# Block sums of weights on VectorE, normed rows kept in memory, layer 1's modulation weights in the row buffers

## The chip, the cores and the metric

The kernel runs on one core of one Trainium2 chip. The metric is the device time of one execution in microseconds; the time before is the median of three runs. The profile is of one further execution, recorded by the hardware profiler. A core has TensorE (PE; its weight loads are listed as PEld), VectorE (DVE), ScalarE (ACT), GpSimd (POOL) and SyncE (SP), which here only issues DMAs.

## The reference

Two layers of a diffusion backbone in fp32 work on 256 context tokens and 1024 latent tokens with 1024 features. Per layer `i`, for the latent tokens (the context tokens the same with their own modulation, and not at all after layer 0):

```python
mod = silu(c) @ ada_w[i] + ada_b[i]                  # 6 sections: sh1, sc1, g1, sh2, sc2, g2
h = x * (1 + sc1) + sh1
m = mixers(h)                                        # GLA, retention, latent attention
x = layer_norm(ALPHA * x + g1 * (m @ w_out), ln1)
u = conv3((x * (1 + sc2) + sh2) @ ffn_up)            # 1024 -> 2 x 2816, a convolution over 3 tokens
f = (silu(u[:2816]) * u[2816:]) @ ffn_down
x = layer_norm(ALPHA * x + g2 * f, ln2)
```

The modulation weights `ada_w[i]` are 1024 x 6144, so 24 MB per layer for a product with two vectors.

## The kernel before

Activations lie transposed: features on the partitions, tokens along the free axis, so 1024 features are 8 row blocks "k". Every fp32 product is made of three fp32r products: each operand is split into a rounded part (a cast on ACT, L255) and the remainder (a subtraction on VectorE, L256), by `split`. Weights are split too, when they are used.

Per layer come the projection, the mixers, the output projection (`wout`), and then the feed-forward stage, which the change touches. The tokens go through it in two parts (`PARTS`, L78): 644 and 636 tokens in layer 0, 512 and 512 in layer 1. The hidden features are 22 blocks of 128, twice (a and g).

- **Up** (`ffn_up`, L1214). One call makes the blocks f (A) and NF + f (G) of the up projection for one part as one 2x2 block product with seven instead of eight multiplications. It needs sums of blocks of the weights (`wload`, L202: x and z, four additions of 128x512 on GpSimd, L218) and sums of blocks of the tokens (`sums`, L1178, the operand X). Seven `product` calls (L1238, matmuls L1242) go through PSUM banks 0 to 3. VectorE and ACT evacuate them (L1251, L1260, L1264, L1257, L1267), then the convolution (L1281 to L1283) and the gate (L1286, L1287) follow, and the result is split.
- **Down** (`ffn_down`, L1292). After three up blocks (first after one) their share of the down projection goes through PSUM banks 4 to 7 (matmuls L1318), is scaled by ACT (L1328) and added to the rows `yd` in memory by a DMA that GpSimd issues (L1330). The order of the calls is in `ffn_order` (L43): a down group follows the first up block of the next group.
- **Background work.** `net.bg` is a list of generators. `tick` advances the first of them, a step or two after every up call and one per step of a down group. After the output projection it holds the LayerNorm of part 1 (`ln`, L1106), in layer 0 then layer 1's modulation (`ada`, L291), and later the second LayerNorm of part 0.
- **Layer 1's modulation** (`ada`). Each of six sections loads eight tiles of 128x1024 (L301), multiplies each with the two vectors (L306, into bank 7, which is also a down bank), and then copies, transposes and stores the section (L310, L314, L319). Before a down group, an unfinished section is brought to its end (`while net.ada_on`).

Buffers are shared by tag: `wst` has 4 slots of 4 KB per partition, for weights as they arrive (A, G, down weights, and the modulation weights). `y` has 8 slots of 5 KB: the rows before and after the first LayerNorm (four slots for each part; those of part 0 are given up when X is made), half of X's split operands (two slots), the block sums x and z (two slots per up block). Part 1's rows, once normed, are stored to `yd` (L1147) and also stay in their `y` slots. `modulate` (L332, on VectorE at L340) scales and shifts them there in place; it is put into the background list at up block 20 of part 0 (`stage[1]`, L1505), and its end is waited for before part 1's first up block (L1499).

The program text does not fix the order on an engine: a scheduler in the framework puts each engine's instructions in order by the text's order, operands and free slots, and then each engine works through its list in that order. The list is fixed before the run.

Of the kernel before, what the change touches and what calls it, by code (L numbers as in the profile page):

```python
# [42 lines left out]
def ffn_order(l):  # L43
    out, pend = [], None
    for part in range(2):
        for gi, (f0, gn) in enumerate(groups(l, part)):
            for f in range(f0, f0 + gn):
                out.append(("up", part, f))
                if pend:
                    out.append(("down",) + pend)  # L50
                    pend = None
            pend = (part, gi)
    return out + [("down",) + pend]
# [7 lines left out]
def groups(l, part):  # L61

    out, f = [], 0
    for n in [1] + [3] * 7:
        out.append((f, n))
        f += n
    return out
# [15 lines left out]
class Net:  # L83
# [118 lines left out]
    def wload(self, i):  # L202

        nc, (src, shape) = self.nc, self.wq[i]
        if not isinstance(src, tuple):
            t = self.ws(shape)
            nc.sync.dma_start(t[:], src)
            self.wst[i] = t
        elif shape == PAIR[0]:
            l, _, f = src  # L210
            A, G = self.ws([128, 8, 128]), self.ws([128, 8, 128])
            nc.sync.dma_start(A[:], self.a["up"][l, f])
            nc.sync.dma_start(G[:], self.a["up"][l, NF + f])
            x, z = self.yk(shape=(128, 2, 4, 128)), self.yk(shape=(128, 2, 4, 128))
            lo, hi = slice(0, 4), slice(4, 8)
            for out, p, q, op in ((x[:, 0], G[:, lo], G[:, hi], ALU.add), (x[:, 1], x[:, 0], A[:, lo], ALU.subtract),
                                  (z[:, 0], A[:, lo], G[:, lo], ALU.subtract), (z[:, 1], A[:, hi], x[:, 1], ALU.subtract)):
                nc.gpsimd.tensor_tensor(out, p, q, op=op)  # L218
            self.wsum[src] = {0: (A, A[:, lo]), 1: (A, A[:, hi]), 2: (z, z[:, 1]), 3: (G, G[:, hi]), 4: (x, x[:, 0]), 5: (x, x[:, 1]), 6: (z, z[:, 0])}

    def wahead(self):
# [1161 lines left out]
def kernel(ctx: ExitStack, tc: tile.TileContext, a, out):  # L1383
    net = Net(ctx, tc, a)
    nc = tc.nc
# [4 lines left out]
    for l in range(NL):  # L1390
# [10 lines left out]
        if l == 0:  # L1401
# [23 lines left out]
            ada = net.after(net.ada(0, [(None, s) for s in (2, 3, 4, 5)]))  # L1425
# [29 lines left out]
        y = [net.ytiles(c1 - c0) for c0, c1 in parts]  # L1455
        yd = net.dp.tile([128, 8, T], F32, name=f"y{l}")

        def residual(part):
            F = []
            c0, c1 = parts[part]  # L1460
            get = net.loader(S.m, c0, c1)
            for k in range(8):
                f = net.hid([128, 644])
                F.append(get(k, f))
                nc.sync.dma_start(y[part][k], xsrc[:, k, c0:c1])
            return F

        P = [net.ffn_part(l, i) for i in range(2)]
        lns = [net.ln(l, p.c0, p.c1, y[p.part], V_LN1G, V_LN1B, (yd, 0)) for p in P]
        Ff = [[], []]  # L1470
        stage = [net.modulate(l, 3, p.c0, p.c1, lambda k, f, p=p: y[p.part][k], Ff[p.part], here=True) for p in P]
        F = residual(0)
        h = net.hsplit(F, parts[0][1] - parts[0][0])
        F1 = residual(1)
# [11 lines left out]
        X = net.sums(Ff[0], P[0].c1 - P[0].c0)  # L1486
        Ff[0] = y[0] = None
        net.after(lns[1])
        if l == 0:
            ada = net.after(net.ada(1, [(None, s) for s in range(6)]))  # L1490
        nx = None
        F = []
        store = [(net.xs, 0), (out, CTX)][l]
# [1 line left out]
        for op, part, x in ffn_order(l):  # L1495
            p = P[part]
            if op == "up":
                if part and x == 0:
                    net.drain(stage[1])  # L1499
                    X = net.sums(Ff[1], p.c1 - p.c0)  # L1500
                    Ff[1] = y[1] = None
                net.ffn_up(l, p, x, X)
                net.tick(2 if ada in net.bg else 1)
                if part == 0 and x == 20:
                    net.bg.insert(0, stage[1])  # L1505
            else:
                while net.ada_on:
                    net.tick()
                for _ in net.ffn_down(l, p, x, yd):
                    net.tick(1, but=ada)  # L1510
                if part == 0 and x == len(groups(l, part)) - 1:
                    net.bg.insert(0, ln2[0])
                if part and x == len(groups(l, part)) - 2:
                    if l == 0:
                        net.drain(ln2[0])
                        nx = net.modulate(1, 0, 0, 640, net.loader(net.xs, 0, 640), F)
                        for _ in nx:
                            pass
                    else:
                        d0, d1 = p.done  # L1520
                        p.Y = net.ytiles(d1 - d0)
                        for k in range(8):
                            nc.sync.dma_start(p.Y[k], yd[:, k, d0:d1])
# [103 lines left out]
```

## Time and profile before

| | us |
|---|---|
| median of 3 runs | 3760.41 (3749.32 to 3762.21) |
| the profiled execution | 3756.62 |
| its span, first to last instruction | 3754.8 |
| TensorE matmuls busy | 3381.9 (90%) |
| TensorE weight loads busy | 2951.0 (79%) |
| VectorE busy | 2710.2 (72%) |
| ACT busy | 1909.6 (51%) |
| GpSimd busy | 1160.8 (31%) |

Layer 0's feed-forward lies at about 940 to 2060 us of the span, layer 1's at about 2870 to 3740. A busy share is a mean over stages with different limits. In a group of instructions "mean ns of one" is the mean duration; what stands behind the second bar is the idle time of that engine just before these instructions, and what ended it. TensorE's busy time is modelled from pipelined matmuls and grows when its granted clock is low.

### The profile page before, as it was taken

The numbers are of one execution on the slowest core, as the hardware profiler recorded it, in microseconds if no ns is written. First come the engines' busy times: TensorE is split into PE (matmuls) and PEld (weight loads), VectorE is DVE, ScalarE is ACT, GpSimd is POOL, SyncE is SP. The second block draws the span as 40 slices with busy tenths as digits, with TensorE's granted clock in tenths as the row PEclk, the third lists the DMA queues.
The fourth block names the chain that finished last, engine by engine and source line by source line (L and its number), as shares of the span: only waits on it lengthen the run. The fifth ranks groups of instructions, "written<-read, shape, count | busy, mean of one in ns | idle before, by whom it ended". The sixth has DMA issues, their size and how long they took to land. (4 is left out here: it accounts for less than half of the span.)

```text
span 3754.8 us, 63790 instructions
## 1 busy us (share of the span) xinstructions
PE 3381.9 (90%) x24510; PEld 2951.0 (79%) x24510; DVE 2710.2 (72%) x4501; ACT 1909.6 (51%) x3785; POOL 1160.8 (31%) x1227
## 2 busy tenths in 40 slices
PE   7999999999888878788998899999998799888997
PEld 6887667679777768688998898767687688787997
DVE  3335878776886655677877744878869899978885
ACT  3334555553454444456555544555545555655554
POOL 0000334330343323235342100333303554445443
PEclk9999999999899988899999999999999999999998
DMA  7554111223345556465455644111232555455553
GB/s 270 174 184 125 37 52 40 75 88 112 94 131 141 146 138 147 110 144 132 119 124 142 217 133 137 32 53 47 66 121 90 132 135 132 113 152 132 122 135 91
DMA packets 223986, 447.60 MB, mean 119 GB/s; under 512 B 20992, under 2 KB 115008, under 8 KB 223680
## 3 DMA queue, kind: packets, MB, share of 16 engines
q1 hardware_dynamic: 187968, 370.11, 30.3%
q0 software_dynamic: 35712, 73.41, 12.8%
q8 instruction: 192, 3.15, 0.3%
q14 instruction: 114, 0.93, 0.1%
HBM read 319.45 MB, written 119.27 MB: 117 GB/s over the span
## 5 line engine op out<-in xcount | busy, mean ns | idle before, releaser
L256 DVE TENSOR_TENSOR w<-ws,w 128x512 fp32r<-128x512 f32 (+2 forms) x476 | 479.1, 1007 | 397.9 <-ACT w L255 137.7
L1242 PE MATMUL ps<-h,w 128*128 128x256 f32 (+2 forms) x4224 | 648.8, 305 | 114.7 <-DVE u L1251 37.3
L1242 PEld LDWEIGHTS ps<-h,w 128*128 128x128 f32 x4224 | 598.4, 195 | 141.4 <-DVE u L1251 44.6
L1318 PE MATMUL ps<-hid,w 128*128 128x256 f32 (+4 forms) x3696 | 615.7, 327 | 60.4 <-ACT t L1328 47.5
L1318 PEld LDWEIGHTS ps<-hid,w 128*128 128x128 f32 x3696 | 567.7, 199 | 98.7 <-ACT t L1328 55.8
L366 PE MATMUL ps<-h,w 128*128 128x320 f32 (+4 forms) x3264 | 549.2, 327 | 11.9 <-ACT h L255 6.3
L366 PEld LDWEIGHTS ps<-h,w 128*128 128x128 f32 x3264 | 509.3, 191 | 52.8 <-issue 15.4
L255 ACT CAST w<-ws 128x512 fp32r<-128x512 f32 (+2 forms) x476 | 361.9, 761 | 259.0 <-PE ps L366 99.8
L1008 POOL TENSOR_SCALAR dg<-ident,sm 128x128 f32<-128x128 f32 x144 | 99.8, 698 | 961.8 <-DVE sm L1006 840.2
L256 DVE TENSOR_TENSOR w<-y,w 128x512 fp32r<-128x512 f32 x352 | 302.6, 864 | 97.0 <-ACT w L255 95.4
L1242 PE MATMUL ps<-hid,w 128*128 128x256 f32 (+2 forms) x2112 | 335.3, 308 | 15.8 <-ACT t L1257 9.5
L962 PE MATMUL ps<-h,h 96*128 96x512 f32 (+1 forms) x1200 | 321.8, 389 | 18.3 <-DVE w L990 13.4
L1242 PEld LDWEIGHTS ps<-hid,w 128*128 128x128 f32 x2112 | 308.6, 199 | 26.8 <-ACT t L1257 11.8
L1330 POOL DMA_DIRECT2D y<-t x248 | 222.2, 1015 | 306.2 <-ACT t L1328 303.8
L255 ACT CAST w<-y 128x512 fp32r<-128x512 f32 x352 | 216.8, 617 | 163.7 <-POOL y L218 72.3
L1328 ACT ACTIVATE t<-ps,mod 128x256 f32<-128x256 f32 (+6 forms) x432 | 211.1, 535 | 113.7 <-PE ps L1318 62.1
L975 ACT ACTIVATE w<-ps,sm 128x768 f32<-128x768 f32 (+2 forms) x272 | 209.1, 774 | 111.5 <-DVE sm L971 89.5
L962 PEld LDWEIGHTS ps<-h,h 96*128 96x128 f32 x1200 | 197.7, 192 | 77.4 <-issue 21.0
L218 POOL TENSOR_TENSOR y<-ws 128x512 f32<-128x512 f32 x88 | 136.4, 1550 | 373.1 <-DMA ws<-in_up_dram 282.9
L988 PE MATMUL ps<-ident,w 128*128 128x128 f32 x1312 | 219.8, 284 | 12.2 <-ACT w L975 11.9
L1281 ACT ACTIVATE t<-u,vec 128x644 f32<-128x644 f32 (+3 forms) x176 | 153.3, 871 | 134.7 <-DVE u L1251 118.0
L988 PEld LDWEIGHTS ps<-ident,w 128*128 128x128 f32 x1312 | 149.7, 142 | 71.1 <-issue 34.6
(225 smaller groups left out, 5538.1 us busy)
## 6 DMA issues: line engine op xcount, KB each, us to landing
ws<-in_up_dram SPq DMA_DIRECT2D x176, 512.0 KB, 4.0
ws<-in_down_dram SPq DMA_DIRECT2D x112, 384.0 KB, 3.2
ws<-in_ada_dram SPq DMA_DIRECT2D x80, 512.0 KB, 3.9
ws<-in_w_in_dram SPq DMA_DIRECT2D x48, 512.0 KB, 4.5
y<-t POOLq DMA_DIRECT2D x64, 321.5 KB, 5.4
y<-t POOLq DMA_DIRECT2D x64, 318.5 KB, 7.4
ws<-in_w_out_dram SPq DMA_DIRECT2D x32, 512.0 KB, 3.4
y<-t POOLq DMA_DIRECT2D x64, 255.5 KB, 6.4
```

Source lines behind the costliest of these rows:

```text
L218: nc.gpsimd.tensor_tensor(out, p, q, op=op)
L255: self.nc.scalar.copy(hi, src)
L256: self.nc.vector.tensor_tensor(lo, src, hi.bitcast(F32), op=ALU.subtract)
L366: nc.tensor.matmul(ps[:, i, 0:n], w_[:, k, :], h[k][:, part, o:o + n], start=(k == 0 and q == 0), stop=(k == 7 and q == 2))
L962: nc.tensor.matmul(sc[:, o:o + n], q[qa][0:96, qs], K[ka][0:96, o:o + n], start=(x == 0), stop=(x == 2))
L975: nc.scalar.activation(P[:, c0:c1], sc[:, c0:c1], AF.Exp, bias=st[:, 2:3], scale=MSCALE, accum_out=st[:, 3 + j:4 + j])
L988: nc.tensor.transpose(ps[:, t_], P[:, 128 * (t0 + t_):128 * (t0 + t_) + 128], self.ident[:])
L1242: nc.tensor.matmul(bank[:, 0:w], w_[:, k, :], X[i][k][:, part, :], start=(first and k == 0 and q == 0), stop=(k == 3 and q == 2), skip_gro ...
L1281: nc.scalar.activation(v[:, 0:n], u[:, 1:1 + n], AF.Identity, scale=cw(j, 1), bias=self.vec[l][:, V_CB + j:V_CB + j + 1])
L1318: nc.tensor.matmul(pb[i][:, 0:n], w[w_][:, x, ms], p.hh[f0 + x][hp][:, o - 1:o - 1 + n], start=(x == 0 and q == 0), stop=(x == gn - 1 and ...
L1328: nc.scalar.activation(t[:, cd - base:cd - base + n], pb[i][:, o:o + n], AF.Identity, scale=self.md(l, 5, m, who))
L1330: nc.gpsimd.dma_start(yd[:, m, base:base + e], t[:, 0:e], accum_op=ALU.add)
```

## The change

Three edits. The four block sums of a weight pair are instructed on VectorE instead of GpSimd. Part 1's normed rows are no longer kept in `y` slots from the LayerNorm on: their tiles are given up when the LayerNorm has stored them, and a new step at block 20 takes four new `y` slots, loads the rows from `yd` with eight DMAs on SyncE, and modulates them there. Layer 1's modulation weights are loaded into `y` slots instead of `wst` slots.

```diff
@@ wload
-                nc.gpsimd.tensor_tensor(out, p, q, op=op)
+                nc.vector.tensor_tensor(out, p, q, op=op)
@@ tile_hybrid_kernel
-        stage = [net.modulate(l, 3, p.c0, p.c1, lambda k, f, p=p: y[p.part][k], Ff[p.part], here=True) for p in P]
+
+        def second():
+
+            p = P[1]
+            Y = net.ytiles(p.c1 - p.c0)
+            for k in range(8):
+                nc.sync.dma_start(Y[k], yd[:, k, p.c0:p.c1])
+            yield
+            yield from net.modulate(l, 3, p.c0, p.c1, lambda k, f: Y[k], Ff[1], here=True)
+
+        stage = [net.modulate(l, 3, P[0].c0, P[0].c1, lambda k, f: y[0][k], Ff[0], here=True), second()]
@@
         net.after(lns[1])
+        lns, y[1] = None, None
         if l == 0:
-            ada = net.after(net.ada(1, [(None, s) for s in range(6)]))
+            ada = net.after(net.ada(1, [(None, s) for s in range(6)], alloc=lambda s: net.yk(shape=s)))
@@
                     X = net.sums(Ff[1], p.c1 - p.c0)
-                    Ff[1] = y[1] = None
+                    Ff[1] = None
```

## Rows read from the trace of the kernel before

**Rows 1.** The page's first part: busy us, share of the span, instructions.
```profile
PE 3381.9 (90%) x24510; PEld 2951.0 (79%) x24510; DVE 2710.2 (72%) x4501; ACT 1909.6 (51%) x3785; POOL 1160.8 (31%) x1227
```
**Rows 2.** Feed-forward stretches: us, busy PE, PEld, DVE, ACT, POOL; PEclk, DMA share, GB/s.
```profile
940.00:2060.00 1120.00, 959.79 (x6201) 906.46 (x6200) 804.21 (x1171) 564.04 (x995) 407.08 (x432) 0.92 0.53 130
2870.00:3740.00 870.00, 758.81 (x5334) 708.40 (x5335) 744.23 (x1114) 496.07 (x904) 400.94 (x439) 0.95 0.52 125
```
**Rows 3.** The same for one group each: layer 0 parts 0, 1; layer 1 parts 0, 1.
```profile
1227.00:1306.30 79.30, 67.47 (x465) 61.87 (x464) 48.49 (x70) 35.42 (x64) 26.63 (x32) 0.91 0.58 147
...
1881.90:1943.40 61.50, 59.24 (x400) 58.47 (x399) 46.00 (x65) 34.42 (x60) 26.42 (x26) 1.00 0.51 120
...
3176.80:3226.40 49.60, 47.12 (x326) 43.43 (x325) 44.70 (x65) 29.72 (x52) 25.45 (x32) 1.00 0.54 137
...
3553.30:3606.40 53.10, 48.81 (x401) 47.81 (x400) 44.56 (x65) 31.44 (x60) 25.05 (x26) 1.00 0.56 131
```
**Rows 4.** TensorE's waits, 1147.6 to 1590: us in total, times, longest.
```profile
PE ps L306 <- DMA ws<-in_ada_dram: 66.2, 24, 4.0
```
**Rows 5.** TensorE in order of time, one section: start, us, instructions, idle before.
```profile
1155.74 0.64 PE L306 MATMUL ps<-ws,st 128*32 128x256 f32 x8 [2.41 <-DMA ws<-in_ada_dram]
1160.27 1.08 PE L306 MATMUL ps<-ws,st 128*32 128x256 f32 x8 [3.88 <-DMA ws<-in_ada_dram]
...
1166.65 0.69 PE L314 MATMUL ps<-ident,t 128*128 128x128 f32 x2 [0.49 <-ACT t L310]
```
**Rows 6.** SyncE's queue in order of time, the same section.
```profile
1147.70 14.04 SPq L301 DMA_DIRECT2D ws<-in_ada_dram  x4
```
**Rows 7.** Line 218: min/median/max ns of the first sum; what ended its idle time.
```profile
L218 POOL TENSOR_TENSOR y<-ws x88: 1256/1322/3196, 958.6 to 3678.6; 128x512 f32<-128x512 f32 x88
...
  DMA ws<-in_up_dram: 282.9, 52
```
**Rows 8.** Line 256, min/median/max ns, of the split of block sums.
```profile
L256 DVE TENSOR_TENSOR w<-y,w x352: 671/684/3949, 963.6 to 3691.7; 128x512 fp32r<-128x512 f32 x176
```
**Rows 9.** All engines in order of time, around one block sum in layer 1.
```profile
3143.16 1.57 POOL L218 TENSOR_TENSOR y<-y,ws 128x512 f32<-128x512 f32 x1
...
3143.24 2.05 DVE L256 TENSOR_TENSOR w<-y,w 128x512 fp32r<-128x512 f32 x1
```
**Rows 10.** VectorE's groups of the whole run: busy us, mean ns, idle before.
```profile
L256 DVE TENSOR_TENSOR w<-y,w 128x512 fp32r<-128x512 f32 x352 | 302.6, 864 | 97.0 <-ACT w L255 95.4 <-PE ps L1242 0.7
L1283 DVE SCALAR_TENSOR_TENSOR t<-u,vec,t 128x644 f32<-128x644 f32 (+3 forms) x176 | 189.7, 1078 | 1.1
L1282 DVE SCALAR_TENSOR_TENSOR t<-u,vec,t 128x644 f32<-128x644 f32 (+3 forms) x176 | 184.1, 1046 | 12.3 <-ACT t L1281 11.1
```
**Rows 11.** VectorE's groups by form, feed-forward of layer 0, then of layer 1.
```profile
L256 DVE TENSOR_TENSOR w<-ws,w 128x512 fp32r<-128x512 f32 x132 | 115.6, 876 | 93.1 <-ACT w L255 91.9
...
L256 DVE TENSOR_TENSOR w<-ws,w 128x512 fp32r<-128x512 f32 x131 | 124.3, 949 | 41.7 <-ACT w L255 41.5
```
**Rows 12.** Line 1282: min/median/max ns.
```profile
L1282 DVE SCALAR_TENSOR_TENSOR t<-u,vec,t x176: 731/877/1997, 987.5 to 3702.6; 128x644 f32<-128x644 f32 x44, 128x638 f32<-128x638 f32 x44, 128x512 f32<-128x512 f32 x44, 128x514 f32<-128x514 f32 x44
```
**Rows 13.** TensorE's waits for evacuations on VectorE, whole run.
```profile
PE ps L1242 <- DVE u L1251: 37.3, 38, 4.2
PE ps L1242 <- DVE t L1260: 31.1, 15, 7.2
```
**Rows 14.** Line 340, modulation: min/median/max ns, first and last start; idle until.
```profile
L340 DVE TENSOR_SCALAR hid<-hid,mod x48: 405/474/615, 17.4 to 2166.4; 128x256 f32<-128x256 f32 x16, 128x384 f32<-128x384 f32 x16, 128x640 f32<-128x640 f32 x16
L340 DVE TENSOR_SCALAR y<-y,mod x40: 397/532/2223, 939.5 to 3036.1; 128x512 f32<-128x512 f32 x16, 128x256 f32<-128x256 f32 x8, 128x388 f32<-128x388 f32 x8, 128x636 f32<-128x636 f32 x8
...
  DMA hid<-xs: 15.2, 7
  DMA hid<-in_xT_dram: 7.7, 4
```
**Rows 15.** DMA issues: KB each, median us from issue to landing, of normed rows.
```profile
y<-y SPq DMA_DIRECT2D x8, 318.5 KB, 5.7
```

## The prediction

> **What bounds the kernel now.** I read the page's engine totals first [rows 1]: TensorE is busy 90% of the span, VectorE 72%, GpSimd 31%. All three edits act in the feed-forward stages, so the second view is the busy time by stretch over these two stages [rows 2]: VectorE is busy 804 of 1120 us in layer 0 and 744 of 870 us in layer 1. The third view is the same table for single groups, each of three up blocks and one down group [rows 3]. In layer 0 a group of part 0 takes 79.3 us, one of part 1 61.5 us. Both compute the same; the group of part 0 also carries one section of layer 1's modulation weights (L306). Its TensorE is busy 67.5 us and idle 11.8, at a granted clock of 0.91; in part 1 it is 59.2 us busy and 2.3 idle, at 1.00. In layer 1 the groups take 49.6 us (47.1 busy) and 53.1 us (48.8 busy), so a steady group there has only 2.5 to 4.3 us to win.
>
> Then the waits of TensorE [rows 4] and one section in order of time [rows 5]. The reader is to see L306 waiting up to 3.88 us for each of its loads, and on SyncE's queue four of these loads in a row that lasts 14 us [rows 6]: a load waits until the matmuls of the one before have released the staging slot, then takes about 3.9 us, then come about 1 us of matmuls, four times. Over the six sections the wait is 66.2 us in 24 pieces. This is the one large stall that repeats.
>
> **Edit 3, layer 1's modulation weights in the y buffers.** There are 8 y slots. In part 0 the split operands of the running part (X) hold two, the block sums of one up block two, and part 1's normed rows four. Edit 2 frees those four until they are reloaded, so that after LayerNorm six slots serve block sums and modulation weights. When a section is drained, two hold the next block's sums, which leaves up to four for the four loads that now go one after another. They need no longer wait for matmuls, and the staging slots are left to the feed-forward weights.
> - Wait removed: 66.2 us [rows 4].
> - Clock: the section's own TensorE work at full clock is 8 x 0.64 + 0.69 = 5.8 us [rows 5]; the busy time of its group is 67.5 - 59.2 = 8.3 us over that of a group without [rows 3]. The 2.5 us between I put down to the stretch of lower clock that follows the stall (1.08 us against 0.64 for the same eight matmuls): 15 us in six sections.
> - Ceiling: 66 + 15 = 81 us. Check by the groups' lengths: 6 x (79.3 - 61.5 - 5.8) = 72 us.
> - Given back: the first matmul of a section needs the PSUM bank that the down group before it uses, so weights loaded too early sit in slots that the next block's sums want. I charge one load per section, 3.88 x 6 = 23 us, from the ceiling, which leaves 58; I take **60 us gained**. Ends: 20 us (half the loads still in series, and the sums late) and 81 us.
>
> **Edit 1, block sums on VectorE.** 88 up blocks with 4 sums each are 352 instructions of 128x512. On GpSimd the quickest kind has a median of 1.32 us [rows 7]. VectorE does the same shape between SBUF operands in a median of 0.684 us (L256, w<-y) [rows 8], so it gains 352 x 0.684 = 241 us of work.
> What it sheds is seen in [rows 9]: the same subtraction takes 2.05 us while a sum runs on GpSimd. Means against undisturbed lengths, over the whole run: w<-y 352 x (864 - 684) ns = 63 us [rows 8, 10]; w<-ws of 128x512 132 x (876 - 684) + 131 x (949 - 684) ns = 60 us [rows 11]; the convolution steps L1282 and L1283, half of them about 512 wide (shortest 731 ns) and half about 640 (for these I take the median, 877, so 804 on average [rows 12]), 176 x (1046 + 1078 - 2 x 804) ns = 91 us [rows 10]. That is 214 us, without L1287, the LayerNorm's and others. VectorE's total thus rises by at most 27 us.
> [...]
> On the path are VectorE's evacuations: TensorE waits 37.3 + 31.1 = 68 us for L1251 and L1260 [rows 13]. They lose the slow-downs and get blocks of sums in front of them instead; I take 20 us as gain. Against it, a sum waits for its weight load. On GpSimd that wait (282.9 us in 52 pieces [rows 7]) cost nothing; on VectorE, which works through its queue in order, the evacuations and weight splits stand behind it, and TensorE waits for both. The trace has no such wait on VectorE. Its nearest instructions are the modulations behind loads: 15.2 + 7.7 us over 48 of them [rows 14], 0.48 us each, times 88 is 42 us, of which I let a third, 15 us, reach TensorE, as VectorE idles 442 us in the two stages [rows 2]. Net: **5 us gained**. Ends: 41 us gained (if the lines left out shed another 68 us, so 282 less 241, all on the path) and 110 us lost (rival C).
>
> **Edit 2, part 1's rows wait in memory.** Eight more loads of 318 KB in layer 0 and 256 KB in layer 1, 5.7 us each to landing [rows 15], on SyncE's queue among the weight loads, and one more step of the background work. The rows' store exists already. The framework issues an instruction when its operands and slots allow, not where the text has it: part 1's modulation stands at block 20, yet the last of them began at 3036.1 [rows 14], with groups of part 0 running past 3226 [rows 3]. So in layer 1, where no modulation weights want the slots, I expect the reload at once after the LayerNorm, and then the state of before. In layer 0 the modulation weights come first. Hidden by some 190 us of feed-forward, the reload costs **0**. Without that cover it is one batch per layer, 2 x (5.7 + 8 x 0.53 us of modulation [rows 14]) = 20 us lost; the other end is 10 us gained, if the sums get a second pair of slots for a while and one wait per group of layer 1's part 0 is halved.
>
> **Sum.** 60 + 5 + 0 = 65 us. The profiled execution took 3756.6 us (span 3754.8 and 1.8 around it), 3.8 us under the median of 3760.4 and within the runs' 3749.3 to 3762.2. 3756.6 - 65 = **3692 us**.
>
> **Rivals.**
> - A, the slots are fought over: modulation weights and block sums take turns on the y slots, and loads stay in series. For it: 6 slots for up to 4 sum tiles and 8 loads of a section, and early issue. Against it: six is more than the one staging slot in use now. It gives the low end of edit 3: 3757 - 20 - 5 = 3732 us.
> - B, more than forecast: the whole stall goes (81) and VectorE's net relief is all on the path (41): 3757 - 122 = 3635 us. For it: TensorE's short waits are on VectorE [rows 13]. Against it: [rows 3] leave steady groups only 2.5 to 4.3 us.
> - C, VectorE becomes layer 1's bound. It now idles 126 us there [rows 2]; 44 blocks bring 44 x 4 x 0.684 = 120 us. If the relief does not come, or is eaten by waiting for loads, the idle time, which is waiting in order, does not fill up and the stage grows by up to 120 us; layer 0 keeps its gain less 10. 3757 - 60 + 120 + 10 = 3827 us; halfway, 3767. It decides from the point where 65/88 = 0.74 us of delay per up block reaches TensorE. For it: the tight row of layer 1 in [rows 2]. Against it: [rows 9].
> - D, the change does not do what it says: the reloaded rows take the four slots back before the modulation weights can use them, so that these compete with the sums for two. 3757 +- 15 us. Against it: in the kernel's text the modulation weights stand before the reload, so they are served first.
>
> **How the numbers follow.** Forecast (3660 to 3725) 0.55, A 0.10, B 0.12, C 0.14, D 0.09. The range 3640 to 3770 leaves out part of B (0.07) and most of C (0.12). A difference of 0.5%, 19 us, is what a measurement of this kernel can tell from none: faster is below 3742. Forecast, A and B are there, 0.77; D is the same, with a little of C, 0.10; the rest of C is slower, 0.13.
>
> **What would show it.** Right: TensorE's wait of L306 for modulation loads in layer 0's feed-forward falls from 66 to under 25 us; groups of part 0 last 66 to 70 us, with the clock near 1.00; SyncE issues L301 without the 14 us row. w<-y at a mean near 0.69 us, with VectorE's total busy time within 40 us of 2710; GpSimd under 700 us. Layer 1's groups within 2 us of 49.6 and 53.1. Wrong: VectorE waiting for up-weight loads by more than 60 us in total, or layer 1's groups longer by over 2 us (C); L306 still waiting more than 45 us (A or D); the sums waiting for slots that modulation weights hold.

## The result, and the profile after

The changed kernel takes 3664.74 us (median of 4 runs, 3663.23 to 3669.04) against 3761.31 for the kernel before on the same chip: a ratio of 0.975, 95% interval 0.9727 to 0.9774. It is 97 us faster. The forecast of 3692 us was 27 us too slow; the range held the time. Its total came near by errors that offset each other; of its terms only edit 3's came near in size, and that with the sums still on GpSimd, as the experiments show.

The page of the kernel after, first part, answers to [rows 1]:

```profile
PE 3371.0 (92%) x24510; PEld 2954.0 (81%) x24510; DVE 2631.2 (72%) x4853; ACT 1916.0 (52%) x3785; POOL 618.0 (17%) x875
```

VectorE took over 352 instructions and yet is 79 us less busy than before. The same feed-forward stages by stretch, as in [rows 2]:

```profile
940.00:1990.00 1050.00, 949.68 (x6227) 901.58 (x6226) 778.65 (x1352) 568.98 (x999) 129.55 (x256) 0.95 0.55 142
2800.00:3655.00 855.00, 762.01 (x5354) 719.13 (x5353) 695.46 (x1295) 501.48 (x905) 141.77 (x264) 0.94 0.54 130
```

Single groups, as in [rows 3]: layer 0 part 0 twice, layer 0 part 1, layer 1 part 0, layer 1 part 1.

```profile
1144.60:1217.40 72.80, 67.69 (x464) 62.32 (x463) 46.91 (x82) 35.22 (x64) 7.67 (x20) 0.93 0.60 160
1217.40:1288.20 70.80, 67.25 (x464) 62.68 (x464) 46.98 (x82) 35.27 (x64) 7.66 (x20) 0.95 0.61 164
1816.60:1877.00 60.40, 58.62 (x399) 58.09 (x398) 45.48 (x77) 34.67 (x60) 7.51 (x14) 1.00 0.54 122
...
3107.50:3160.60 53.10, 48.92 (x325) 45.67 (x325) 41.39 (x77) 30.27 (x52) 7.70 (x20) 0.94 0.56 129
3424.70:3476.70 52.00, 48.59 (x396) 48.38 (x395) 41.77 (x77) 31.47 (x60) 7.52 (x14) 0.97 0.57 131
```

Three groups are shorter than before; the group of layer 1's part 0 is 3.5 us longer (53.1 against 49.6), at a granted clock of 0.94 where it was 1.00. What it waits for is in VectorE's waits of the kernel after; the kernel before has no such row on VectorE:

```profile
DVE y L218 <- DMA ws<-in_up_dram: 149.5, 53, 7.3
```

And in order of time, in layer 1's part 0:

```profile
3027.35 0.69 DVE L218 TENSOR_TENSOR y<-ws 128x512 f32<-128x512 f32 x1 [4.90 <-DMA ws<-in_up_dram]
...
3030.36 0.42 DVE L1251 TENSOR_TENSOR u<-ps,t 128x256 f32<-128x256 f32 x1
...
3030.84 1.65 PE L1242 MATMUL ps<-h,w 128*128 128x256 f32 x6 [4.60 <-DVE u L1251]
```

The first sum of a block stands at the head of VectorE's list and waits 4.9 us for its weights. The evacuation L1251 stands behind it, with two more sums and two splits between, and TensorE waits 4.6 us for that evacuation. The pattern returns in five groups there: TensorE waits 4.0 to 4.7 us for L1251 at 2978.1, 3030.8, 3084.2, 3136.3 and 3189.4 us, and in none of the groups before.

TensorE's waits after, during layer 1's modulation in layer 0's feed-forward (1090 to 1530 us), and of the whole run:

```profile
PE ps L306 <- DMA y<-in_ada_dram: 21.7, 25, 3.1
```

```profile
PE ps L1242 <- DVE u L1251: 47.3, 19, 4.8
...
PE ps L1242 <- DVE t L1260: 25.3, 16, 4.6
PE ps L1318 <- ACT t L1328: 16.9, 14, 2.8
```

The modulation loads cost 21.7 us where they cost 66.2 [rows 4]; the first section reads so in order of time, against [rows 5]: one load is still waited for, and three are all but there.

```profile
1149.56 0.64 PE L306 MATMUL ps<-y,st 128*32 128x256 f32 x8 [0.34 <-DMA y<-in_ada_dram]
1153.33 1.08 PE L306 MATMUL ps<-y,st 128*32 128x256 f32 x8 [3.13 <-DMA y<-in_ada_dram]
1154.61 1.08 PE L306 MATMUL ps<-y,st 128*32 128x256 f32 x8 [0.20 <-DMA y<-in_ada_dram]
1155.86 1.08 PE L306 MATMUL ps<-y,st 128*32 128x256 f32 x8 [0.17 <-DMA y<-in_ada_dram]
```

### The profile page after: what moved, and what is told of

The parts are those of the page before. It is cut to its first block, busy times and chain, and to the rows that moved or that the text cites. A ratio compares the mean times of both kernels' runs of the same rounds, so it can differ in the third digit from the quotient of the medians.

```text
span 3667.3 us, 63639 instructions
## 1 busy us (share of the span) xinstructions
PE 3371.0 (92%) x24510; PEld 2954.0 (81%) x24510; DVE 2631.2 (72%) x4853; ACT 1916.0 (52%) x3785; POOL 618.0 (17%) x875
## 5 line engine op out<-in xcount | busy, mean ns | idle before, releaser
L1242 PE MATMUL ps<-h,w 128*128 128x256 f32 (+2 forms) x4224 | 651.2, 306 | 104.9 <-DVE u L1251 47.3
L1242 PEld LDWEIGHTS ps<-h,w 128*128 128x128 f32 x4224 | 605.1, 197 | 125.5 <-DVE u L1251 52.5
L256 DVE TENSOR_TENSOR w<-ws,w 128x512 fp32r<-128x512 f32 (+2 forms) x476 | 411.0, 865 | 342.2 <-PE ps L366 146.0
L1318 PE MATMUL ps<-hid,w 128*128 128x256 f32 (+4 forms) x3696 | 600.8, 323 | 34.1 <-ACT t L1328 16.9
L1242 PE MATMUL ps<-hid,w 128*128 128x256 f32 (+2 forms) x2112 | 338.8, 309 | 22.4 <-ACT t L1257 13.0
L1242 PEld LDWEIGHTS ps<-hid,w 128*128 128x128 f32 x2112 | 311.5, 200 | 33.4 <-ACT t L1257 14.4
L1330 POOL DMA_DIRECT2D y<-t x248 | 215.2, 896 | 472.8 <-ACT t L1328 470.7
L256 DVE TENSOR_TENSOR w<-y,w 128x512 fp32r<-128x512 f32 x352 | 240.6, 688 | 36.9 <-ACT w L255 34.1
L1328 ACT ACTIVATE t<-ps,mod 128x256 f32<-128x256 f32 (+6 forms) x432 | 209.2, 534 | 105.3 <-PE ps L1318 65.6
L1225 POOL MEMSET u<- 128x1 f32 (+1 forms) x264 | 27.3, 156 | 1151.3 <-DVE t L1283 811.0
```

Of the source, the lines that this page charges most:

```text
L256: self.nc.vector.tensor_tensor(lo, src, hi.bitcast(F32), op=ALU.subtract)
L1242: nc.tensor.matmul(bank[:, 0:w], w_[:, k, :], X[i][k][:, part, :], start=(first and k == 0 and q == 0), stop=(k == 3 and q == 2), skip_gro ...
L1318: nc.tensor.matmul(pb[i][:, 0:n], w[w_][:, x, ms], p.hh[f0 + x][hp][:, o - 1:o - 1 + n], start=(x == 0 and q == 0), stop=(x == gn - 1 and ...
L1328: nc.scalar.activation(t[:, cd - base:cd - base + n], pb[i][:, o:o + n], AF.Identity, scale=self.md(l, 5, m, who))
L1330: nc.gpsimd.dma_start(yd[:, m, base:base + e], t[:, 0:e], accum_op=ALU.add)
```

## The experiments

All were timed against the kernel before (3760 to 3762 us in each set) on one chip per set. "Shift" below is how much earlier (negative) an up block begins than in the kernel before, in the profiled runs: the start of the L1242 matmul that stands at n/88 of that line's records. The 88 up blocks are counted from 0 in order of time: block 22 is the first of layer 0's part 1, block 44 the first of layer 1, block 66 the first of its part 1. "End" is the end of the span. Each row is one profiled run.

| shift, us | block 22 | block 44 | block 66 | end |
|---|---|---|---|---|
| edit 1 alone | -8.5 | -29.4 | -52.9 | -78.4 |
| edit 2 alone | +9.0 | +10.9 | +14.3 | +7.7 |
| edits 1 and 2 | -15.8 | -28.3 | -21.1 | -48.4 |
| edits 2 and 3 | -37.9 | -50.3 | -40.5 | -43.9 |
| all three | -44.2 | -67.3 | -59.8 | -87.6 |
| all three, every third block's sums on GpSimd | -51.1 | -82.4 | -90.4 | -117.6 |
| all three, edit 2 in layer 0 only | -47.4 | -74.5 | -101.9 | -128.6 |
| both | -58.3 | -98.1 | -111.5 | -139.1 |

**One edit, or two.** The first four runs took the change apart. Edit 3 without edit 2 was not tried: the rows that stay and the modulation weights want the same slots.

Edit 1 alone:

```diff
-                nc.gpsimd.tensor_tensor(out, p, q, op=op)
+                nc.vector.tensor_tensor(out, p, q, op=op)
```

> Edit 1 alone (block sums on VectorE; rows and modulation weights as before). Before 3761 us, after 3665 us. Theory S (the serial loads of modulation weights are most of the gain, about 70 of 97 us): about 3740 us; L306 still waits about 66 us in layer 0's feed-forward, w<-y falls to a mean of 0.69 us, VectorE waits over 100 us for up weights. Theory P (the GpSimd contention is most of it): 3700 us or less, with layer 0's groups of part 0 at 75 us or less instead of 79.3.

Measured: 3676.66 us, ratio 0.9775 (0.9752 to 0.9799), 84 us faster by itself. Theory S fell. Theory P had the time, but not the place: up to layer 0's part 1 the run gains only 8.5 us. TensorE's waits of the kernel before, and then of this one:

```profile
PE ps L1318 <- ACT t L1328: 47.5, 28, 6.1
...
PE ps L1242 <- DVE t L1264: 18.3, 18, 2.4
```

```profile
PE ps L306 <- DMA ws<-in_ada_dram: 81.5, 43, 4.1
PE ps L1242 <- DVE t L1260: 26.4, 16, 4.0
PE ps L1318 <- ACT t L1328: 17.4, 13, 2.2
PE ps L1242 <- DVE u L1251: 16.9, 8, 3.7
...
PE ps L1242 <- DVE t L1264: 5.1, 3, 4.1
```

With [rows 13], four waits lose 30 (L1328), 20 (L1251), 13 (L1264) and 5 us (L1260): 68 us. TensorE's busy time falls as well, from 3381.9 to 3369.4 us, and some other waits are longer; the spans differ by 78 us. The sums wait 67.8 us for weights on VectorE, and little of it shows in the evacuations.

Edit 2 alone (the diff of the change without its first line pair and without `alloc=`):

> Edit 2 alone (part 1's rows reloaded; sums on GpSimd, modulation weights through the staging slots). Theory S: 3761 within 8 us, since the reload is hidden and freed slots alone start nothing that was late. Theory Q (the freed slots let the block sums run a pair ahead): 3740 us or less, and GpSimd's sums wait less for w L256.

Measured: 3765.08 us, ratio 1.0015 (0.9999 to 1.0031): no change.

Edits 1 and 2:

```diff
-            ada = net.after(net.ada(1, [(None, s) for s in range(6)], alloc=lambda s: net.yk(shape=s)))
+            ada = net.after(net.ada(1, [(None, s) for s in range(6)]))
```

> Edits 1 and 2, without edit 3. Theory S: about 3735 us, so that edit 3 is worth about 70 us on top; L306 waits about 66 us. Theory P: 3690 us or less. Theory Q: 20 us or more below edit 1 alone.

Measured: 3701.83 us, 0.9848 (0.9824 to 0.9871). None of the theories had named this time. Edit 2, which costs nothing alone, costs 25 us beside edit 1. The table says where: from block 44 to 66, edit 1 alone gains 23.5 us, and both together lose 7. In that stretch this kernel has five of the stalls for L1251 shown above (4.1 to 4.7 us each), and edit 1 alone has none. VectorE's waits for up weights, edit 1 alone and edits 1 and 2:

```profile
DVE y L218 <- DMA ws<-in_up_dram: 67.8, 29, 6.8
...
DVE y L218 <- DMA ws<-in_up_dram: 120.8, 40, 6.9
```

Edits 2 and 3, sums on GpSimd:

```diff
-                nc.vector.tensor_tensor(out, p, q, op=op)
+                nc.gpsimd.tensor_tensor(out, p, q, op=op)
```

> Edits 2 and 3, block sums still on GpSimd. Theory S: about 3690 us; layer 0's groups of part 0 fall from 79.3 to about 72 us, layer 1's part 0 stays at 49.6 us per group (the 52.5 us of after come from the sums on VectorE waiting for weights). Theory P: 3730 us or more.

Measured: 3709.95 us, 0.9868 (0.9833 to 0.9903), 55 us less than edit 2 alone, between what the two theories had named. Edit 3's gain arrives before block 44. From block 44 to 66 this kernel loses 10 us and edit 2 alone 3, so a small part of edit 2's loss there may not need the sums on VectorE. TensorE's wait for L1328 is 45.5 us here, as before the change, so its fall belongs to edit 1.

So edit 1 gives 84, edit 3 55 and edit 2 loses 5; the sum would be 134, and the change has 97. Edit 3's part shrinks too: beside edits 1 and 2 it is worth 37 us (3701.83 against 3664.74).

**What the sums on GpSimd cost.** The changed kernel with twelve additions per up block on GpSimd (three after each sum), whose results nothing reads:

```diff
+                for j in range(3):
+                    nc.gpsimd.tensor_tensor(self.dgt()[:], G[:, j], A[:, j], op=ALU.add)
```

> The changed kernel, with twelve idle additions of 128x128 per up block put on GpSimd beside the sums on VectorE (their results are not used; they read the same weights). This brings back GpSimd's traffic and nothing else. If GpSimd's additions slow VectorE's: w<-y rises from a mean of 0.69 to 0.8 us or more, VectorE's busy time by 100 us or more over 2631, and the time to 3690 us or more. If GpSimd's traffic does not matter: all three stay within 1%.

Measured: 3857.8 us, 1.0251 (1.0234 to 1.0267), 193 us over the changed kernel. GpSimd's busy time is 1389.9 us, VectorE's 2844.2, which is 213 more than after, for the same instructions. Its groups of VectorE (lines two further on than after: L258 is L256, L1284 is L1282):

```profile
L258 DVE TENSOR_TENSOR w<-ws,w 128x512 fp32r<-128x512 f32 (+2 forms) x476 | 445.1, 937 | 337.2 <-PE ps L368 138.9 <-ACT w L257 72.9 <-PE ps L499 64.3
L258 DVE TENSOR_TENSOR w<-y,w 128x512 fp32r<-128x512 f32 x352 | 266.9, 762 | 38.7 <-ACT w L257 37.4 <-PE ps L1244 0.2
```

The same groups after:

```profile
L256 DVE TENSOR_TENSOR w<-ws,w 128x512 fp32r<-128x512 f32 (+2 forms) x476 | 411.0, 865 | 342.2 <-PE ps L366 146.0 <-ACT w L255 76.0 <-PE ps L497 63.9
L256 DVE TENSOR_TENSOR w<-y,w 128x512 fp32r<-128x512 f32 x352 | 240.6, 688 | 36.9 <-ACT w L255 34.1 <-PE ps L1242 1.3
```

Beside work on GpSimd that nobody needs, VectorE's instructions took those 213 us more, though the mean of w<-y, 762 ns, stays under the 800 that were expected. TensorE's wait for L1328 rises to 70.9 us as well, so this run does not separate the slowing of VectorE from the accumulating DMAs (L1330) that stand behind the sums in GpSimd's list. One run takes away the length and keeps GpSimd's wait for the weights:

```diff
+            nc.gpsimd.tensor_tensor(self.dgt()[:, 0:1], G[:, 0, 0:1], A[:, 0, 0:1], op=ALU.add)
```

> The changed kernel with one more instruction on GpSimd per up block: an addition of 128x1 that reads the first column of both weight tiles, into a tile that nothing reads. It makes GpSimd's list wait for the weights' landing, as the sums did before the change, and takes next to no time on the memory that VectorE uses. Theory 1: a good part of edit 1's gain is that the accumulating DMAs (L1330) no longer stand behind a GpSimd that waits for weights; then TensorE's wait of the down matmuls (L1318) for ACT's scaling (L1328) rises from 16.9 towards 47.5 us, and the time by 20 to 30 us, to 3685 to 3695 us. Theory 2: what GpSimd's sums cost was their running time, beside VectorE and in front of those DMAs; then the wait stays under 25 us and the time within 8 us of 3665 us.

Measured: 3679.12 us, 0.979 (0.9771 to 0.981), 14 us over the changed kernel's run, in another set. GpSimd's row and TensorE's waits (lines one further on than after):

```profile
POOL dg L219 <- DMA ws<-in_up_dram: 660.3, 82, 86.1
```

```profile
PE ps L1243 <- DVE u L1252: 58.6, 19, 6.2
...
PE ps L1319 <- ACT t L1329: 19.7, 14, 4.7
```

GpSimd waits for weights far longer than it did before the change (282.9 us [rows 7]), and TensorE's wait for ACT's scaling rises only from 16.9 to 19.7. Theory 1 falls: waiting in GpSimd's list does not bring the 30 us back, and its time of 3685 us or more is not reached. Theory 2's bound of 8 us on the time is not settled: the profiled spans differ by 8 us, the medians by 14, and the intervals touch. TensorE's evacuation wait is 11 us longer (58.6 against 47.3), with the sums on VectorE waiting 171.4 us instead of 149.5; why one small instruction does that stays open. What remains for the 30 us is the sums' running time, in the list or by slowing VectorE and with it everything up to the scaling; no run tells these two apart.

The traces speak for the list. Each accumulating DMA can be set against the end of the last scaling that feeds it. Before the change GpSimd issues the 248 of them late by 473 us in all, 69 of them by more than 3 us; 311 us of this pass while its sums run and 53 us while it waits for weights. After the change it is 90 us in all and none is over 3 us late. With the small instruction it is 169 us (10 over 3 us), of which 56 are waits for weights: about as much waiting as before the change, with hardly any running (19 us). With the twelve additions it is 805 us (110 over 3 us). ACT's scaling waits for the tiles that these DMAs read, before and after:

```profile
ACT t L1328 <- DMA y<-t: 35.9, 15, 5.7
...
ACT t L1328 <- DMA y<-t: 21.4, 15, 3.4
```

**What the waiting on VectorE costs.** The sums read the constant `ident` instead of the weight tiles, so they wait for no load; the block products with sums are then not those of the reference:

```diff
+                i4 = cap(self.ident, 0, [[0, 4], [1, 128]])
+                nc.vector.tensor_tensor(out, i4, i4, op=op)
```

> The changed kernel with block sums that read a constant tile in place of the weights (so the block sums are not the weights' sums): same instructions on VectorE, no wait for a weight load. If the wait behind loads costs time on VectorE: VectorE's 149 us of waits for up weights go, layer 1's groups of part 0 fall from 52.5 to 49 us or less, and the time to 3640 us or less. If it is the added work and not the wait: 3665 within 8 us.

Measured: 3573.98 us, 0.9506 (0.9483 to 0.9528), 91 us less than the changed kernel, with VectorE as busy as there (2630.0 us). If nothing else hangs on it, some 60% of the 149.5 us of waiting reach the end. Two runs try to get at it.

The sums of every third up block, the one that stalls in layer 1's groups, on GpSimd:

```diff
+                (nc.gpsimd if src[2] % 3 == 1 else nc.vector).tensor_tensor(out, p, q, op=op)
```

> The changed kernel, but the sums of every third up block (the one whose sums make TensorE wait for L1251 in layer 1) are back on GpSimd. If the waiting in VectorE's queue is what costs layer 1's part 0 its 3 us per group: groups of 49.6 us again, and 3645 us or less. If contention costs as much as it saves: 3665 within 8 us.

Measured: 3636.09 us, 0.9658 (0.9631 to 0.9686), 29 us faster than the change. VectorE's wait for weights falls from 149.5 to 83.0 us; 137.1 us of waiting move to GpSimd.

The sums of a block queued on VectorE behind the evacuations of the g half of the block before (main part of the edit; the rest also holds back the splits that need these sums):

```diff
+        last = plus(U[1], 0, b3, s6)
+        self.early = False
+        while self.late:
+            self.late.pop(0)[1](last)
```

> The changed kernel, but in VectorE's queue the next block's sums stand behind the present block's evacuations L1251 of the g half (by order alone, with no wait added). If the evacuations queued behind waiting sums are the cost: TensorE's waits for L1251 fall from 47 us to under 20, layer 1's groups of part 0 to about 49 us, and the time to 3640 us or less. If the later sums make the next block late instead: 3665 us or more.

Measured: 3759.23 us, 0.9995 (0.9983 to 1.0008): the whole gain is gone, although the sums now wait only 10.5 us for weights. TensorE waits 83.2 us for the evacuation L1260 (25.3 in the change). A later place for the sums does not help as such; how much of this the splits cost that were held back with them was not tried.

**Where the lost 37 us are.** In edit 1 alone, part 1's rows hold four y slots, and the sums have to wait for slots. With edit 2 they find them free; the theory is that they then stand earlier in VectorE's list, ahead of their weights. If so, edit 2 should be kept to layer 0, where the modulation weights need it:

```diff
-        stage = [..., second()]
+        stage = [..., second() if l == 0 else net.modulate(l, 3, P[1].c0, P[1].c1, lambda k, f: y[1][k], Ff[1], here=True)]
-        lns, y[1] = None, None
+        lns = None
+        if l == 0:
+            y[1] = None
-                    Ff[1] = None
+                    Ff[1] = y[1] = None
```

> The changed kernel with edit 2 in layer 0 only: in layer 1 part 1's normed rows stay in their y slots, as before the change. Theory: in layer 1 the freed slots let the sums stand earlier in VectorE's list, in front of evacuations and ahead of their weights' landing, which costs a stall of some 4.6 us per group of part 0. Kept slots hold the sums back until the weights are there. Then layer 0 is as in the changed kernel, layer 1's part 0 takes some 30 us less (as in the run with edit 1 alone, where it ended 23.5 us earlier against the kernel before instead of 7 us later), VectorE's wait for up weights falls from 149.5 to some 105 us, and the time is 3630 to 3645 us. Rival: the stall in layer 1 has another cause (the reload's DMAs among the weight loads, or a state carried over from layer 0); then the time stays within 10 us of the changed kernel's 3665 us.

Measured: 3635.92 us, 0.9668 (0.9648 to 0.9687), 29 us faster than the change and inside the expected 3630 to 3645. Waits of this kernel's VectorE, and one of its groups of layer 1's part 0:

```profile
DVE y L218 <- DMA ws<-in_up_dram: 108.9, 39, 6.4
```

```profile
3067.80:3115.10 47.30, 46.90 (x327) 43.44 (x326) 41.67 (x78) 30.16 (x51) 7.67 (x20) 1.00 0.62 146
```

The group is 5.8 us shorter than in the change at the same VectorE work (41.67 against 41.39 us), and TensorE is idle for 0.4 us of it. VectorE's list in order of time, at the block of the group that stalls in the change:

```profile
3054.43 0.42 DVE L1251 TENSOR_TENSOR u<-ps,t 128x256 f32<-128x256 f32 x1
...
3055.69 0.69 DVE L218 TENSOR_TENSOR y<-ws 128x512 f32<-128x512 f32 x1
3056.30 0.42 DVE L1251 TENSOR_TENSOR u<-ps,t 128x256 f32<-128x256 f32 x1
3056.64 0.68 DVE L218 TENSOR_TENSOR y<-y,ws 128x512 f32<-128x512 f32 x1
3057.24 0.42 DVE L1251 TENSOR_TENSOR u<-ps,t 128x256 f32<-128x256 f32 x1
...
3061.59 0.69 DVE L218 TENSOR_TENSOR y<-ws,ws 128x512 f32<-128x512 f32 x1
3062.20 0.69 DVE L218 TENSOR_TENSOR y<-ws,y 128x512 f32<-128x512 f32 x1
```

In the change three sums stand ahead of the first of the three L1251 of the block before. Here the first sum stands behind it and the second pair behind all three, one pair for each slot that comes free, and no sum waits. The weights come earlier too: the two loads of that block are issued 11.6 and 15.7 us after the group's first sum (16.5 and 17.7 in the change). But counted from the evacuation L1264, right behind which the first sum stands in the change, the second load lands 3.7 us later here and 5.3 us later in the change. In the change's place the sum would have waited here too, so the place in the list is the larger part; the rest was not told apart.

The run also takes the reload out of layer 1, so by itself it does not rule out that the reload's loads hold up the weights. The trace of the changed kernel does: SyncE issues the first of these loads at 3178.70 us, when four of the five stalls are over.

```profile
3178.70 12.12 SPq L1477 DMA_DIRECT2D y<-y  x6
```

The last store of part 1's rows, which frees the slots, is issued at 2944.2 us, and the stalls begin at 2978.1. The table agrees: up to block 44 this kernel is within 8 us of the change, then it gains 27 us while the change loses 7.5. The three gains nearly add now: 126 us of 134.

Both together, edit 2 in layer 0 only and every third block's sums on GpSimd:

> The run before (edit 2 in layer 0 only) and the block sums of every third up block back on GpSimd. If the third's 28 us gain came mainly from the blocks that stall in layer 1's part 0, it is already had by keeping the slots, and the time is within 10 us of the run before (some 3635 us). If it came from fewer waits for weights in VectorE's list everywhere (layer 0 ended 15 us earlier with it), the two add up in part, and the time is 3605 to 3625 us.

Measured: 3624.67 us, 0.9639 (0.962 to 0.9659), the fastest that was run, 137 us under the kernel before. Its interval overlaps that of the run before it, so the 11 us between are not settled. By the table, the third's sums on GpSimd gained 15 us up to block 44 and 15 more in layer 1's part 0, where the stall is. With the slots kept there they gain 24 us up to block 44 and lose 14 again in that part. So about half of the third's 29 us was the same stall.

## Why the prediction was right and wrong

**Edit 3, 60 us gained: right with the sums on GpSimd, too large beside edit 1.** Measured 55 (edits 2 and 3 against edit 2), and 37 beside edits 1 and 2; why it is worth less there stays open. The wait of L306 fell from 66.2 to 21.7 us, under the 25 named, and the one load per section charged as given back (23 us) is about what is left. The clock came back only in part: of the loads whose eight matmuls stand alone, eight of 24 still take 1.08 us (15 of 26 took over 1 us before), the group's clock is 0.93 to 0.95, not near 1.00, and the groups take 70.8 to 72.8 us, not 66 to 70. Rivals A and D are out.

**Edit 1, 5 us gained: the failed step.** By itself it gave 84 us. The step "I take 20 us as gain" of TensorE's 68 us of waits for L1251 and L1260 was mis-sized, and its base was too small: 25 us of those two went, and 43 us of two waits that were not in the sum, L1328 (30) and L1264 (13). Even the bound "if the lines left out shed another 68 us" (282 us shed, 41 gained) was too low: VectorE shed 241 + 79 = 320 us, not 214. w<-y is at 688 ns as forecast; VectorE's total fell by 79 us, outside the 40 named. [Rows 9] had shown that GpSimd's sums slow VectorE (2.05 us for one subtraction, against a median of 0.684 [rows 8]); what the prediction did not do was to follow them to every wait of TensorE, and it had no term for the DMAs that stand behind the sums in GpSimd's list. The run with idle additions shows the slowing too, 213 us of VectorE's time for some 770 us of GpSimd's. Rival C had VectorE become layer 1's bound, from its 126 us of idle time there [rows 2]. VectorE's busy time in that stage fell instead, from 744 of 870 us to 695 of 855, because it was partly GpSimd's doing.

**The wait for weights, 15 us lost: too small.** Priced at 42 us by the modulations' waits [rows 14], it is 149.5 us on VectorE, and the run without it is 91 us faster. "VectorE waiting for up-weight loads by more than 60 us" was named as the sign of rival C, and it came; layer 1's groups of part 0 are 3.5 us longer, as C had it. But C's price was wrong, since the relief came as well and was larger.

**Edit 2, 0: right alone, wrong beside edit 1.** Its step "in layer 1 I expect the reload at once after the LayerNorm, and then the state of before" failed. The line of the modulation in the kernel after:

```profile
L340 DVE TENSOR_SCALAR y<-y,mod x40: 401/536/898, 941.4 to 3209.7; 128x512 f32<-128x512 f32 x16, 128x256 f32<-128x256 f32 x8, 128x388 f32<-128x388 f32 x8, 128x636 f32<-128x636 f32 x8
```

The last one began at 3209.7 us, near the end of part 0, where it was at 3036.1 before [rows 14], and the reload itself was not issued before 3178.70. So the sums had four more slots through most of layer 1's part 0. The prediction saw this as its good end ("the sums get a second pair of slots", 10 us gained); it cost 29 us. That the total came out near is luck: edit 1's gain, taken 79 us too small, met this loss, some 37 us with what else does not add and taken as none, and 5 us each in edits 2 and 3 (edit 2's within the noise): 65 + 79 - 37 - 10 = 97.

## What to carry to other kernels

Elementwise work on GpSimd was not free here, 213 us of VectorE's time for 772 us of its own: price it by what VectorE's instructions beside it lose against their undisturbed lengths, and follow these, and the DMAs that wait behind it in GpSimd's list, to every wait of the bounding engine, not to two of them. Before work that waits for a load is put into the list of an engine with evacuations behind it, ask what holds it back until the load has landed. Free buffers took that brake away in layer 1 here, for 29 us. Where a change gains in one stage and loses in another, try it without the stage that lost.

## What the runs showed of the hardware

Moving 241 us of VectorE-length work from GpSimd to VectorE made VectorE less busy by 79 us. 542 us less GpSimd time per run was worth 84 us in all by edit 1 alone, with sums that wait for their weights on VectorE; GpSimd time added to the changed kernel for nothing cost 193 us for 772 us. DMAs that GpSimd issues stood behind its running sums: 248 of them were late by 473 us in all with the sums there, and by 90 without. Layer 1's part 0 with five stalls of 4.0 to 4.7 us (2800 to 3209 us of the changed kernel) had a granted clock of 0.93 and TensorE busy for 354.9 us; with edit 2 in layer 0 only and no such stall (2793 to 3167 us) it was 0.98 and 342.3 us for the same work.
